# An encoder block on one core: inputs laid out on the host and loaded in fewer pieces, and another order of work at its two ends

## The chip, the cores and the metric

The kernel runs on one core of one Trainium2 chip. A core has a matrix engine (TensorE, PE in the profile, with its weight loads as PEld), a vector engine (VectorE, DVE), an activation engine (ScalarE, ACT), a general engine (GpSimd, POOL) and a sequencer that does little but issue loads and stores (SyncE, SP). ACT and POOL can issue loads too. The metric is the time of one execution on the device in microseconds (us), the median of several runs; less is better.

## The reference

One block of an encoder on a sequence of 256 tokens with 2048 channels, all in float32. Cut to what matters:

```python
hn = rmsnorm(h, mix_norm_pre)                      # h = x at first, (256, 2048)
z, xbc, dt_raw, u = split(hn @ w_in)               # 1024, 1536, 32 and 1024 columns
y_ssd = ssd_mixer(z, xbc, dt_raw, ...)             # centred conv over 5 tokens, scan both ways, gate by z
y_pool = pool_mixer(u, pool_w, pool_scale)         # means over 2, 4, 8, 16 tokens, a linear map
mix = concat([y_ssd, y_pool]) @ w_out
h = h + rmsnorm(mix, mix_norm_post)
ff = conv_glu(rmsnorm(h, ffn_norm_pre), ...)       # 2048 -> 2 x 5632, conv over 3 tokens, gelu, -> 2048
h = h + rmsnorm(ff, ffn_norm_post)
gate = sigmoid(rmsnorm(h, ple_norm_pre) @ w_ple_gate)
return h + rmsnorm(gate * (p @ w_ple), ple_norm_post)
```

`rmsnorm` divides each token's row by the root of its mean square (plus 1e-6) and multiplies each channel by a gain.

## The kernel before

Every product is made of float32 parts. A weight tile is loaded as it is (`raw`), ACT casts it to the format that PE takes (`hi`, line 160), DVE takes the difference (`lo`, line 161), and PE sums three products: x hi by w hi, x hi by w lo, x lo by w hi. `split` (lines 156 to 162) does this; its `hi` and `lo` tiles turn over in five buffers each (`whi`, `wlo`), so that the sixth cast waits for PE to be done with the first. The activations are kept with channels along the partitions in a `Panel`: 16 k-tiles of 128 channels by 256 tokens, `hi` and `lo`, made by `put` (lines 193 to 198: ACT scales by the channel's gain, DVE makes the rest). The row's root is applied behind the product.

The order of work comes from the program's text, with a scheduler that lets later instructions go earlier where their inputs allow; `tc.issue_after` holds one behind another. Nearly all loads are issued on SP's queue, in order, by `load` (lines 115 to 118); one that waits for a buffer holds all behind it. Buffers: `raw` three, `page` (2048 floats a partition) thirteen, `mid` three; PSUM has six banks in `main` and two in `misc`.

The stages, in order:

- Start (lines 92 to 153). POOL makes `ident`, the unit matrix; PE runs nine transposes of it into an unused bank (line 103) while the first loads are under way. `x` is loaded with tokens along the partitions, two token halves, 256 or 512 columns at a time (`xload`), on SP. The gain and convolution vectors are loaded as rows of 128 (`vrow`): one on ACT's queue, nine on POOL's, which also loads `mask`, `dtb`, `alog` and `dsk`. `vturn` transposes the rows on PE and DVE copies them into the columns of `vt`; `vec(i)` is one column.
- `dtu` (lines 346 to 375): the columns of `w_in` for dt and u, 1056 of them, 16 k-tiles. `panel_part` (line 286) transposes `x` on PE, two transposes a k-tile (line 293), and `put` reads the result from PSUM. For each k-tile 18 matmuls of 352 columns go into six banks: two token halves, three products, three column blocks. The raw tiles are `dtur`.
- Row sums and what depends on them (lines 377 to 441): `row_rstd` squares the rows of `x` on ACT; `p` is loaded, transposed on PE and split (`pth`, `ptl`); then dt is made from the first bank by a chain of small DVE instructions that ends in `dah` and `dal` (lines 440, 441).
- `xbc` and `z` (lines 523 to 614): the rest of `w_in`. Between their weight tiles stand the jobs in `work`: `seg_prep` (POOL, products `ap` from `dah`), `seg` (PE and ACT), `pool_mix`, `pool_map` and so on. Each of three slabs of `xbc` ends in a convolution on DVE (line 341).
- The output projection, the feed-forward part (`ga`, `va`, `dna` in the profile) and the small product `ple`.
- The gate (lines 753 to 801): `token_major` with `w_ple_gate`, two halves of 1024 columns. A weight pair is two k-tiles in one load. For all pairs but the last `tail` ones, PE does its matmuls as each pair comes; the last `tail` pairs are done together at the end, bank by bank: first token half 0, then token half 1 (line 226). With `tail = 1 + half` the second half of the columns keeps two pairs, four k-tiles, for this end. Token half 1 has its second bank cut into two of 256 columns, the last one in `gtz`. After each bank: tanh (ACT, line 791), plus one and times `pl` (DVE, 792), square with a sum along the row (ACT, 795), times the gain (DVE, 796). `finish` takes the row's root from POOL (`rms`: one small instruction a partial sum, then a power) and adds `h`: three of four chunks on DVE (line 774), chunk 2 by ACT (771) and POOL (772); each chunk is stored on SP (776).

Of the kernel before, what the change touches and what calls it, by code (L numbers as in the profile page):

```python
# [51 lines left out]
def build(nc, a, out):  # L52
    x, p = a["x"][0], a["p"][0, 0]
# [3 lines left out]

    def rows(ap):
        return ap.rearrange("(n p) -> n p", p=P)

    with tile.TileContext(nc) as tc, \
# [8 lines left out]
        def ins(r):  # L70
            return getattr(r, "ins", r)
# [26 lines left out]
        nc.scalar.activation(tiny("tables", 1), mhalf[:, 0:1], AF.Exp)  # L98
# [3 lines left out]
        for i in range(9):  # L102
            nc.tensor.transpose(warm[:, :P], ident, ident)
        xt = [page(f"x{t}") for t in range(2)]
        vrow = page("vrow")
        vr = vrow[:, :4 * P].rearrange("p (c f) -> p c f", c=4)

        def vload(eng, ch, r0, src, n):
            eng.dma_start(vr[r0:r0 + n, ch, :], src)

        vload(nc.scalar, 0, 0, rows(a["mix_norm_pre"][0]), 16)
# [8 lines left out]
        def xload(c0, c1):  # L120
            for t in range(2):
                last["dma"] = load(xt[t][:, c0:c1], x[t * P:(t + 1) * P, c0:c1])

        xload(0, 256)
        vload(nc.gpsimd, 3, 0, a["ssd_conv_w"][0].rearrange("j (n p) -> (j n) p", p=P), 60)
        vload(nc.gpsimd, 3, 60, rows(a["ssd_conv_b"][0]), 12)
        vload(nc.gpsimd, 3, 72, rows(a["ssd_norm"][0]), 8)
        vload(nc.gpsimd, 3, 80, rows(a["pool_scale"][0]), 8)
        vload(nc.gpsimd, 3, 88, rows(a["ffn_norm_pre"][0]), 16)
        vload(nc.gpsimd, 1, 0, a["ffn_conv_w"][0, 0:2].rearrange("j (n p) -> (j n) p", p=P), 88)  # L130
        vload(nc.gpsimd, 2, 0, rows(a["ffn_conv_w"][0, 2]), 44)
        vload(nc.gpsimd, 2, 44, rows(a["ple_norm_pre"][0]), 16)
        vload(nc.gpsimd, 2, 60, rows(a["ffn_conv_b"][0]), 44)

        mask = ep.tile([P, 4, P], F32, name="mask")
        nc.gpsimd.dma_start(mask, a["masks"].rearrange("m p f -> p m f"))
        vt = cp.tile([P, V_N], F32, name="vt")
        dtb = ep.tile([P, 32], F32, name="dtb")
        alog = ep.tile([P, 32], F32, name="alog")
        dsk = ep.tile([P, H], F32, name="dsk")  # L140
        nc.gpsimd.dma_start(dtb, a["ssd_dt_bias"][0].rearrange("d h -> (d h)").partition_broadcast(P))
        nc.gpsimd.dma_start(alog, a["ssd_a_log"][0].rearrange("d h -> (d h)").partition_broadcast(P))
        nc.gpsimd.dma_start(dsk, a["ssd_d"][0].partition_broadcast(P))

        def vec(i):
            return vt[:, i:i + 1]

        def vturn(ch, c0, n):
            vps = misc(f"vps{ch}")
            nc.tensor.transpose(vps[:, :n], vr[:n, ch, :], ident[:n, :n])  # L150
            nc.vector.tensor_copy(vt[:, c0:c0 + n], vps[:, :n])

        vturn(0, 0, 16)


        def split(name, src, nel):

            hi = wp.tile([P, 1056], F32R, tag="whi", bufs=5, name=f"{name}h")
            lo = wp.tile([P, 1056], F32R, tag="wlo", bufs=5, name=f"{name}l")
            last["act"] = ins(nc.scalar.copy(hi[:, :nel], src))  # L160
            last["dve"] = ins(nc.vector.tensor_sub(lo[:, :nel], src, hi[:, :nel].bitcast(F32)))  # L161
            return hi, lo
# [184 lines left out]
        front = panel_part("hn", hn, xt, V_MIX, 0, 2)  # L347
        for i in range(9):
            nc.tensor.transpose(warm[:, :P], xt[1][:, 128:256], ident)


        c_dt = DSSD + 1536
        for u in range(0, NK, 2):
            if u % 4 == 0 and u:
                panel_part("hn", hn, xt, V_MIX, u, u + 4)
            r = [wp.tile([P, 2048], F32, tag="raw", bufs=3, name=f"dtur{u}"), page(f"dtur{u + 1}")]
            for j in range(2):
                last["dma"] = load(r[j][:, :1056], w_in[(u + j) * P:(u + j + 1) * P, c_dt:c_dt + 1056])
                if u + j == 0:
                    xload(256, 512)  # L360
                    panel_part("hn", hn, xt, V_MIX, 2, 4)
            if u % 4 == 0 and u < 12:
                xload((u + 4) * P, (u + 8) * P)
            for j in range(2):
                k = u + j
                with tc.issue_after(front[0]), tc.issue_after(front[1]):
                    wh, wl = split(f"dtu{k}", r[j][:, :1056], 1056)
                if k == 8:
                    half = last["act"], last["dve"]
                for t in range(2):  # L370
                    xh, xl = (v[:, t * P:(t + 1) * P] for v in hn(k))
                    for q, (xx, ww) in enumerate(((xh, wh), (xh, wl), (xl, wh))):
                        for n in range(3):
                            o = acc2[t][:, :352] if n == 2 else acc[t][n][:, :352]
                            mm(o, xx, ww[:, n * 352:(n + 1) * 352], k == 0 and q == 0, k == NK - 1 and q == 2)

        with tc.issue_after(half[0]), tc.issue_after(half[1]):
            rx = row_rstd("rx", xt)
            vturn(3, 16, 104)
            vturn(1, 120, 88)  # L380
            vturn(2, 208, 104)
# [8 lines left out]
            pt = page("pt")  # L390
            nc.gpsimd.dma_start(pt[:, :512].rearrange("p (t c) -> p t c", t=2), p.rearrange("(t p) c -> p t c", p=P))
            pth = cp.tile([P, 2, L], F32R, name="pth")
            ptl = cp.tile([P, 2, L], F32R, name="ptl")
            ps = misc("ptp")
            for k in range(2):
                for t in range(2):
                    nc.tensor.transpose(ps[:, (2 * k + t) * P:(2 * k + t + 1) * P],
                                        pt[:, t * 256 + k * P:t * 256 + (k + 1) * P], ident)
            pflat = ps.rearrange("p (k t) -> p k t", k=2)
            nc.scalar.copy(pth, pflat)  # L400
            nc.vector.tensor_sub(ptl, pflat, pth.bitcast(F32))
# [360 lines left out]
        ro = {}  # L762

        def finish(t, cs):
            if t not in ro:
                ro[t] = rms(f"go{t}", sq[t], 1.0 / D)
            r = ro[t]
            for c in cs:
                s = slice(c * 512, (c + 1) * 512)
                if c == 2:  # L770
                    nc.scalar.activation(vg[t][:, s], vg[t][:, s], AF.Identity, scale=r)
                    nc.gpsimd.tensor_add(vg[t][:, s], vg[t][:, s], h[t][:, s])
                else:
                    nc.vector.scalar_tensor_tensor(vg[t][:, s], vg[t][:, s], r, h[t][:, s],  # L774
                                                   op0=ALU.mult, op1=ALU.add)
                nc.sync.dma_start(out[t * P:(t + 1) * P, s], vg[t][:, s])
# [44 lines left out]
```

## Time and profile before

| | |
|---|---|
| Median of three runs | 1166.49 us (1166.0 to 1167.83) |
| The profiled execution | 1168.07 us, with a span of 1165.9 us |
| Granted TensorE clock, mean | 0.993 |
| Loads and stores | 216.94 MB, mean 186 GB/s |
| Groups of matmuls of the feed-forward part (`ga`, `va`, `dna`) | share of the chain of waits: 21% each |

The span runs from the first instruction to the last; the execution's time has about 2 us around it. A group in the profile is named by its line, engine, operation and tiles ("out<-in" by the program's names), with how often it ran. Line 89 is the matmul helper, so matmuls are told apart by their tiles. A time in a timeline is counted from the start of the span; a row has its start, its length, the engine, the line, the operation and, in brackets, how long the engine was idle before and what ended that. A length with "xN" covers N instructions in a row. Matmuls are pipelined: each has a latency longer than the step to the next, so steps are taken from starts.

### The profile page before, as it was taken

To read this page: it belongs to the slowest core of one execution; us is meant where nothing else is said; L and a number is where in the kernel's file an instruction comes from. 1 tells how busy PE (TensorE), PEld (TensorE's weight loads), DVE (VectorE), ACT (ScalarE), POOL (GpSimd) and SP (SyncE) were. 2 spreads that over 40 slices of the span, in tenths; PEclk is the share of its full clock that TensorE was granted. 3 is DMA by queue.
4 is the path that set the end of the run, shared out by engine and by line. 5 is a ranking of instruction groups with operands and counts; after the bars stand their busy time and mean duration, and the time that the engine had idled before them with its cause. 6 is when DMAs were issued, how large, how long until landed. Compare 5 with 4: busy or idle time off the path is not lost.

```text
span 1165.9 us, 15412 instructions
## 1 busy us (share of the span) xinstructions
PE 1143.7 (98%) x6138; PEld 984.0 (84%) x6138; DVE 755.4 (65%) x933; ACT 576.6 (49%) x774; POOL 132.9 (11%) x138
## 2 busy tenths in 40 slices
PE   8998999999999999999999999999999999999995
PEld 8997988888888888888888888888888888887885
DVE  4579797655777665665766756656555565557554
ACT  4634543454575554544544544544444454447453
POOL 2165404300110000000000000000000000001002
PEclk9998999999999999999999999999999999999998
DMA  9653337555465565555555555566566556654742
GB/s 312 239 206 109 109 111 261 208 180 190 134 217 181 188 195 194 182 180 185 194 194 186 181 183 192 183 205 213 182 193 198 185 183 194 198 183 145 248 149 73
DMA packets 129591, 216.94 MB, mean 186 GB/s; under 512 B 3896, under 2 KB 96722, under 8 KB 128880
## 3 DMA queue, kind: packets, MB, share of 16 engines
q1 hardware_dynamic: 128944, 215.23, 56.4%
q0 software_dynamic: 544, 0.72, 0.4%
q8 instruction: 48, 0.79, 0.3%
q14 instruction: 23, 0.19, 0.0%
q10 hardware_dynamic: 32, 0.01, 0.0%
HBM read 213.85 MB, written 2.10 MB: 185 GB/s over the span
## 4 chain that ended last, share of the span: by engine, by line
PE 91%; DVE 5%; ACT 1%; DMA 1%; POOL 1%; issue 1%; SPq 0%; DVEq 0%; POOLq 0%; ACTq 0%
PE va L89 21%; PE dna L89 21%; PE ga L89 21%; PE woa L89 8%; PE gt L89 7%; PE z L89 4%; PE xbc L89 3%; PE dtu L89 3%; DVE cv L341 2%; DMA dtur<-w_in 1%; DVE w L542 1%; DVE xb_0l L161 0%; PE ple L89 0%; PE yd L89 0%; DVE vg L774 0%
## 5 line engine op out<-in xcount | busy, mean ns | idle before, releaser
L89 PE MATMUL ga<-wox,ug_0h 128*128 128x512 f32 x352 | 126.2, 396 | 0.0
L89 PE MATMUL ga<-wox,ug_1h 128*128 128x512 f32 x352 | 125.8, 395 | 0.0
L89 PE MATMUL va<-wox,uv_0h 128*128 128x512 f32 x352 | 125.5, 395 | 0.0
L89 PE MATMUL va<-wox,uv_1h 128*128 128x512 f32 x352 | 125.5, 395 | 0.0
L89 PE MATMUL dna<-dn_1h,hs 128*128 128x512 f32 x352 | 104.5, 394 | 0.0
L89 PE MATMUL dna<-dn_0h,hs 128*128 128x512 f32 x352 | 104.5, 393 | 0.0
L89 PE MATMUL ga<-wox,ug_1l 128*128 128x256 f32 x352 | 99.0, 281 | 0.0
L89 PE MATMUL ga<-wox,ug_0l 128*128 128x256 f32 x352 | 99.0, 281 | 0.0
L89 PE MATMUL va<-wox,uv_0l 128*128 128x256 f32 x352 | 98.9, 281 | 0.0
L89 PE MATMUL va<-wox,uv_1l 128*128 128x256 f32 x352 | 98.9, 281 | 0.0
L89 PEld LDWEIGHTS va<-wox,uv_1h 128*128 128x128 f32 x352 | 66.1, 188 | 15.7
L89 PEld LDWEIGHTS va<-wox,uv_0h 128*128 128x128 f32 x352 | 66.1, 188 | 15.7
L89 PEld LDWEIGHTS ga<-wox,ug_1h 128*128 128x128 f32 x352 | 66.1, 188 | 15.5
L89 PEld LDWEIGHTS ga<-wox,ug_0h 128*128 128x128 f32 x352 | 66.1, 188 | 15.5
L89 PEld LDWEIGHTS dna<-dn_1h,hs 128*128 128x128 f32 x352 | 66.2, 188 | 15.2
L89 PEld LDWEIGHTS dna<-dn_0h,hs 128*128 128x128 f32 x352 | 66.1, 188 | 15.2
L719 POOL TENSOR_TENSOR fc<-fc,rfb 128x1024 f32<-128x1024 f32 x11 | 26.4, 2404 | 443.0 <-ACT fc L718 443.0
L89 PEld LDWEIGHTS ga<-wox,ug_0l 128*128 128x128 f32 x352 | 66.4, 189 | 0.1
L89 PEld LDWEIGHTS ga<-wox,ug_1l 128*128 128x128 f32 x352 | 66.4, 189 | 0.0
L89 PEld LDWEIGHTS va<-wox,uv_1l 128*128 128x128 f32 x352 | 66.4, 189 | 0.0
L89 PEld LDWEIGHTS va<-wox,uv_0l 128*128 128x128 f32 x352 | 66.4, 189 | 0.0
L735 ACT CAST hs<-hid 128x512 fp32r<-128x512 f32 x44 | 27.3, 620 | 71.0 <-PE dna L89 70.7
(644 smaller groups left out, 2674.1 us busy)
## 6 DMA issues: line engine op xcount, KB each, us to landing
dn0r<-w_ffn_down SPq DMA_DIRECT2D x22, 1024.0 KB, 5.4
dn1r<-w_ffn_down SPq DMA_DIRECT2D x22, 1024.0 KB, 5.5
dtur<-w_in SPq DMA_DIRECT2D x16, 528.0 KB, 8.7
zr<-w_in SPq DMA_DIRECT2D x8, 1024.0 KB, 5.1
wo0r<-w_out SPq DMA_DIRECT2D x8, 1024.0 KB, 5.7
wo1r<-w_out SPq DMA_DIRECT2D x8, 1024.0 KB, 5.5
gt0r<-w_ple_gate SPq DMA_DIRECT2D x8, 1024.0 KB, 5.5
gt1r<-w_ple_gate SPq DMA_DIRECT2D x8, 1024.0 KB, 5.5
```

The costliest lines, as they stand in the source:

```text
L89: nc.tensor.matmul(o, lhsT, rhs, start=start, stop=stop, skip_group_check=True)
L341: nc.vector.scalar_tensor_tensor(o[:, lo:hi], i[:, lo + d:hi + d], vec(wcol + j * wstep + f), o[:, lo:hi], op0=ALU.mult, op1=ALU.add)
L542: nc.vector.scalar_tensor_tensor(w[:, h * P:(h + 1) * P], cbm[:, 0, g, t, :], dt[:, t, 8 * g + h:8 * g + h + 1], w[:, h * P:(h + 1) * P], ...
L719: nc.gpsimd.tensor_tensor(cv.rearrange("p (f t) -> p f t", f=4), cv.rearrange("p (f t) -> p f t", f=4), rfb.unsqueeze(1).to_broadcast([P, ...
L735: nc.scalar.copy(t[:, :512], src)
```

## The change

At the start, a host function `laid_out` puts three arrays together by copying: `x_cols`, the 16 gains of the first norm and then `x` transposed into k-tiles of 128 channels by 256 tokens; `p_t`, `p` transposed; `columns`, the other vectors as columns, then `dtb`, `alog`, `dsk` repeated over the partitions, then the four masks. The kernel loads them on SP in few loads (`xt`, `vt`, `small`, `pt`); the `vrow` rows, their transposes, the transposes of `x` (`panel_part` here) and of `p`, and POOL's loads are gone. The row sums load `x` a second time, with tokens along the partitions (`xs_`), behind the last `dtu` weight tile. Weight tile 0 comes in three pieces, two of them issued first on ACT's queue ahead of ACT's table load, the third on SP; tile 1 comes in two. Their casts and differences are cut likewise (`cuts`). For k-tile 0 the matmuls go product by product over both token halves. The warm-up transposes are 16 in place of 9, and the nine behind the first `x` are gone.

At the end, the second half of the gate keeps four pairs in place of two (`1 + 3 * half`); four of those eight k-tiles take their `hi` and `lo` from four pages (`spare`). All final adds are on DVE. For token half 1 POOL sums the partial sums ahead of the last one, takes the root (`rest_of`) and writes it beside the last piece's values, so that the last square's sum is the whole mean square; then one power remains.

```diff
+        c_dt = DSSD + 1536
+        r0 = wp.tile([P, 2048], F32, tag="raw", bufs=3, name="dtur0")
+        for n in range(2):
+            first = ins(nc.scalar.dma_start(r0[:, n * 352:(n + 1) * 352],
+                                            w_in[:P, c_dt + n * 352:c_dt + (n + 1) * 352]))
+        with tc.issue_after(first):
+            nc.scalar.activation(tiny("tables", 1), mhalf[:, 0:1], AF.Exp)
...
-        for i in range(9):
+        for i in range(16):
             nc.tensor.transpose(warm[:, :P], ident, ident)
...
-        vload(nc.gpsimd, 3, 0, a["ssd_conv_w"][0].rearrange("j (n p) -> (j n) p", p=P), 60)
...
-        nc.gpsimd.dma_start(mask, a["masks"].rearrange("m p f -> p m f"))
...
+        last["dma"] = load(xt[0], a["x_cols"][:, :V_SCW + L])
+        dtb, alog, dsk = small[:, :32], small[:, 32:64], small[:, 64:80]
+        mask = small[:, 80:].rearrange("p (m f) -> p m f", m=4)
...
+            for c0, c1 in zip((0, *cuts), (*cuts, nel)):
+                s = slice(c0, c1)
+                last["act"] = ins(nc.scalar.copy(hi[:, s], src[:, s]))
+                last["dve"] = ins(nc.vector.tensor_sub(lo[:, s], src[:, s], hi[:, s].bitcast(F32)))
...
-        front = panel_part("hn", hn, xt, V_MIX, 0, 2)
-        for i in range(9):
-            nc.tensor.transpose(warm[:, :P], xt[1][:, 128:256], ident)
+        def x_panel(k0, k1):
+            for k in range(k0, k1):
+                done = put(hn(k), x_part(k), vec(V_MIX + k))
+            return done
+        front = x_panel(0, 1)
...
+                if k == 0:
+                    last["dma"] = load(r[0][:, 704:1056], w_in[:P, c_dt + 704:c_dt + 1056])
+                    xload(1, 2)
+                    x_panel(1, 2)
+                    continue
+                for c0, c1 in ((0, 704), (704, 1056)) if k == 1 else ((0, 1056),):
+                    last["dma"] = load(r[j][:, c0:c1], w_in[k * P:(k + 1) * P, c_dt + c0:c_dt + c1])
+                if k == 1:
+                    xload(2, 4)
+                elif k in (3, 5, 7):
+                    xload(*{3: (4, 9), 5: (9, 13), 7: (13, 16)}[k])
+                elif k == 4:
+                    load(vt, a["columns"][:, :V_N - V_SCW])
+                elif k == 6:
+                    load(small, a["columns"][:, V_N - V_SCW:])
...
-            rx = row_rstd("rx", xt)
+            xs_ = [page(f"x{t}") for t in range(2)]
+            for t in range(2):
+                load(xs_[t], x[t * P:(t + 1) * P, :])
+            rx = row_rstd("rx", xs_)
...
+        def rest_of(o):
+            base = EPS * D
+            for n, q in enumerate(sq[1]):
+                m = tiny(f"go1m{n}", 1)
+                nc.gpsimd.tensor_scalar(m, q, 1.0, base, op0=ALU.mult, op1=ALU.add)
+                base = m
+            nc.gpsimd.tensor_tensor(o, m, half_up, op=ALU.pow)
...
-                if c == 2:
-                    nc.scalar.activation(vg[t][:, s], vg[t][:, s], AF.Identity, scale=r)
-                    nc.gpsimd.tensor_add(vg[t][:, s], vg[t][:, s], h[t][:, s])
-                else:
-                    nc.vector.scalar_tensor_tensor(vg[t][:, s], vg[t][:, s], r, h[t][:, s],
-                                                   op0=ALU.mult, op1=ALU.add)
+                nc.vector.scalar_tensor_tensor(vg[t][:, s], vg[t][:, s], r, h[t][:, s],
+                                               op0=ALU.mult, op1=ALU.add)
...
+                for i in (8, 6):
+                    sh, sl = page(f"gth{i}", F32R), page(f"gtl{i}", F32R)
+                    for j in range(2):
+                        spare[f"gt1{NK - i}_{j}"] = (sh[:, j * 1024:(j + 1) * 1024], sl[:, j * 1024:(j + 1) * 1024])
-            token_major(f"gt{half}", w_gate, half * 1024, list(range(NK)), hp, acc, 1 + half)
+            token_major(f"gt{half}", w_gate, half * 1024, list(range(NK)), hp, acc, 1 + 3 * half)
```

More of the change, by code (lines that the diff above doesn't have):

```diff
@@ L56, in build @@
     out = out[0]
-    def rows(ap):
-        return ap.rearrange("(n p) -> n p", p=P)
     with tile.TileContext(nc) as tc, \
@@ L138, in build @@
[L138 to L143, printed above, removed]
-        def vec(i):
[L146 to L161, printed above, removed]
+        def x_part(k):
+            return xt[0][:, V_SCW:] if k == 0 else xt[1 + k // 9][:, (k - 1) % 8 * L:((k - 1) % 8 + 1) * L]
@@ L790, in build @@
                     v = th[:, :c1 - c0]
+                    end = half == t == 1 and c1 == 1024
+                    if end:
+                        rest_of(th[:, c1 - c0:c1 - c0 + 1])
                     nc.scalar.activation(v, o, AF.Tanh, scale=rh[t])
```

134 lines of the change are left out of this document (70 added, 64 removed).

## The prediction

> **What bounds the kernel now.** I read the page first, for where the time lies; then the chain of work that ended last, in order of time, because the change touches only the first 60 us and the last 35; then the timelines and the busy time by window of those two ends.
>
> ```profile
> span 1165.9 us, 15412 instructions
> ...
> PE 1143.7 (98%) x6138; PEld 984.0 (84%) x6138; DVE 755.4 (65%) x933; ACT 576.6 (49%) x774; POOL 132.9 (11%) x138
> ```
>
> TensorE (PE) is busy for 98% of the span. So there are two ways to gain: matmuls taken away, and time at either end in which PE waits or has already finished.
>
> ```profile
> 5.46 12.10 DMA dtur<-w_in
> ...
> 43.33 16.45 PE dtu L89 x102
> ...
> 91.29 12.65 DVE cv L341 x15
> ```
>
> In this chain (start, length, what) the first stage, `dtu`, is late once, for the load of its fourth weight tile; then PE runs it alone up to 43.33 + 16.45 = 59.78. Here 102 matmuls take 16.45 us, 0.161 us each; the stage has 16 x 18 = 288 of them, 46.4 us. Much later a convolution on VectorE (DVE) comes on the path.
>
> ```profile
> 0.73 0.86 SPq L118 DMA_DIRECT2D x<-x  x2
> ...
> 1.31 0.79 POOL L109 DMA_DIRECT2D vrow<-ssd_conv_w  x1 [0.34 <-issue]
> ...
> 2.21 0.32 POOL masks.py:199 TENSOR_SCALAR_AFFINE_SELECT ident<-ident 128x128 f32<-128x128 f32 x1
> ...
> 2.58 2.18 PE L103 MATMUL dtu<-ident 128*128 128x128 f32 x9 [2.58 <-POOL ident masks.py:199]
> ...
> 6.61 1.07 ACT L160 CAST dtu0h<-dtur 128x1056 fp32r<-128x1056 f32 x1
> ...
> 7.74 1.24 PE L89 MATMUL dtu<-dtu0h,hnh 128*128 128x352 f32 x6
> ```
>
> This is the timeline of the start. The first useful matmul is at 7.74, behind the load and the whole cast of tile 0. From 7.74 to 59.78 are 52.0 us for 46.4 us of matmuls; the other 5.6 are transposes and waits.
>
> ```profile
> L293 PE MATMUL hnt<-ident,x 128*128 128x128 f32 x32 | 5.9, 295 | 0.0
> ...
> L196 ACT ACTIVATE hnh<-hnt,vt 128x256 fp32r<-128x256 f32 x16 | 7.4, 473 | 17.0 <-PE hnt L293 15.4 <-DVE hnl L197 1.4
> ```
>
> **The change part by part: the front.** All 32 transposes of `x` go, and with them four of `vrow` and four of `p`. Eight of the 32 stand ahead of 7.74, so 24 leave the stage; that is 24 x 0.11 = 2.6 us of the 5.6, by this row of the timeline, (1.03 - 0.295)/7 a step:
>
> ```profile
> 34.25 1.03 PE L293 MATMUL hnt<-ident,x 128*128 128x128 f32 x8
> ```
>
> The other 3.0 are waits for tiles 3 and 4 and for the ScalarE (ACT) step behind the transposes.
>
> When can the first matmul run? It needs `x` tile 0 (136 KB with the gains) and, piece by piece, weight tile 0.
>
> ```profile
> dtur<-w_in SPq DMA_DIRECT2D x1, 528.0 KB, 4.9
> x<-x SPq DMA_DIRECT2D x2, 128.0 KB, 2.5
> ```
>
> Two 128 KB loads landed 2.5 us after issue, the tile issued third, at about 1.6, after 4.9: 784 KB were in by 6.5. Now 664 KB are wanted, and two pieces are issued on ACT's queue beside SP's, so `x` lands at about 3.5 to 4, the third piece between 4.6 (at the 353 GB/s of the window 4 to 6 us, shown below) and 5.9. An ACT step of 0.47 and three casts of a third of 1.07 follow; each is done about 0.4 after its piece. PE is ready before that: POOL no longer issues a load of 0.79 us ahead of the mask that makes `ident`, so the 16 warm-ups, at (2.18 - 0.43)/8 = 0.22 each, end near 5.1 (at 6.1, if `ident` were as late as now). I take 5.8 for the start that the stage would have had if it never waited, between 5.0 and 6.8.
>
> Does it then run through? Up to weight tile 15 the queue carries 16 x 528 KB, 2 MB of `x` and 0.45 MB of vectors and masks: 11.2 million bytes.
>
> ```profile
> 4.00:6.00 2.00, 2.00 (x10) 1.63 (x9) 0.17 (x1) 0.00 (x0) 2.00 (x4) 1.00 1.02 353
> ...
> 14.00:16.00 2.00, 2.00 (x15) 1.98 (x15) 1.64 (x2) 0.71 (x2) 0.00 (x0) 1.00 0.98 113
> ...
> 2.00:18.00 16.00, 15.29 (x88) 13.86 (x88) 6.58 (x10) 6.61 (x12) 6.87 (x14) 1.00 0.99 293
> 18.00:26.00 8.00, 6.75 (x40) 6.44 (x41) 4.48 (x5) 4.61 (x6) 0.00 (x0) 1.00 1.03 410
> ```
>
> The last column is GB/s, the one before it the DMA engines' busy share. At 14 to 16 us they are busy and move almost nothing: the short rows of `mask`, `dtb`, `alog`, `dsk` from POOL's queue are in flight. Once these are through, 410 hold, `x` loads among them. The change merges the short rows into rows of 1 to 5 KB. Even at the 293 of the bad stretch, tile 2 (2.15 MB in the queue's order) is there at 9.4, tile 4 (3.9 MB) at 15.3, tile 7 at 24.2, tile 15 at 40.3. PE wants tile k at 5.8 + 2.9k: 11.6, 17.4, 26.1, 49.3. A cast of 1.07 fits in each time; the tightest is tile 7, by 0.8. ACT has 0.47 + 1.07 = 1.54 us of work for each tile against PE's 2.9, and DVE has the same two steps. The second copy of `x`, 2 MB for the row sums, is queued behind tile 15; ACT's square over it stands ahead of the cast of tile 15, and at 293 GB/s its first half is there at 44. So the stage ends at 5.8 + 46.4 = 52.2 in place of 59.8: **7.6 us**, bounds 6.5 and 8.4.
>
> **The stage behind it.** What matters is not PE alone.
>
> ```profile
> 68.98 0.20 DVE L440 CAST dah<-da 128x64 fp32r<-128x64 f32 x1
> ...
> 91.22 13.45 DVE L341 SCALAR_TENSOR_TENSOR cv<-xr,vt,cv 128x254 f32<-128x254 f32 x16
> ...
> 133.41 6.39 DVE L341 SCALAR_TENSOR_TENSOR cv<-xr,vt,cv 128x254 f32<-128x254 f32 x16
> ```
>
> ```profile
> 69.26 1.07 POOL L465 TENSOR_TENSOR ap<-dah,mask 128x512 fp32r<-128x512 f32 x1 [13.67 <-DVE dah L440]
> 70.31 2.01 POOL L465 TENSOR_TENSOR ap<-dal,mask 128x512 fp32r<-128x512 f32 x1
> ...
> 101.20 1.22 POOL L465 TENSOR_TENSOR ap<-dal,mask 128x512 fp32r<-128x512 f32 x1
> ```
>
> The first convolution runs beside POOL's `ap` products and takes 13.45 us, the second mostly without them 6.39; PE then waits for a PSUM bank that DVE frees behind it:
>
> ```profile
> PE seg L89 <- DVE catl L197: 4.1, 1, 4.1
> ```
>
> After the change the chain to `dah` has two more weight subtractions (`xb`) in front of it, the last of which waits for PE: `dah` comes some 11.8 us after the end of `dtu`, not 9.4, and POOL starts 2.4 later. But the two subtractions that met POOL's first products, two long ones (2.01 against 1.07), are over by then: 2 us back. POOL ends about 0.4 later against the end of `dtu`, the convolution starts 0.8 earlier (seven transposes of 0.11 gone behind `dtu`), and ends where it did. I take 0 here: DVE's chain, and all behind it, moves forward with the end of `dtu`. PE's wait grows by the 0.8 us that it saved. Bounds: 3.9 lost, 4.0 gained (rivals).
>
> **The tail.** PE has the same matmuls in another order, so its end stays; only what follows counts. In the tail the first token half stands ahead of the second; with eight tiles in it in place of four, PE finishes that half 24 matmuls of 512 columns earlier:
>
> ```profile
> 1142.84 5.55 PE gt L89 x24
> ```
>
> Its work on ACT, DVE and POOL moves 5.5 us ahead with it, out of the way of the second half.
>
> ```profile
> 1151.71 1.42 DVE L774 SCALAR_TENSOR_TENSOR vg<-vg,go0r,h 128x512 f32<-128x512 f32 x2 [1.15 <-POOL go0r L283]
> ...
> 1153.69 0.28 PE L89 MATMUL gtz<-gt_1h,dnxl 128*128 128x256 f32 x1
> ...
> 1155.47 0.45 ACT L791 ACTIVATE gth<-gtz,rh 128x256 f32<-128x256 f32 x1
> ...
> 1156.79 0.42 DVE L792 SCALAR_TENSOR_TENSOR gth<-gth,pl 128x256 f32<-128x256 f32 x1
> ...
> 1157.24 0.42 ACT L795 ACTIVATE gth<-gth 128x256 f32<-128x256 f32 x1 [0.28 <-DVE gth L792]
> ...
> 1157.56 0.19 ACT L795 ACTIVATION_READ_ACCUMULATOR gth<-gth 128x1 f32 x1
> ...
> 1158.26 0.55 POOL L283 TENSOR_TENSOR go1r<-go1m,mhalf 128x1 f32<-128x1 f32 x1
> 1158.85 3.08 DVE L774 SCALAR_TENSOR_TENSOR vg<-vg,go1r,h 128x512 f32<-128x512 f32 x3 [1.19 <-POOL go1r L283]
> ```
>
> PE ends at 1153.97, but the last tanh starts at 1155.47, behind DVE's and ACT's work on half 0. Freed of it: tanh 1154.01 to 1154.46, multiply to 1154.90, square and its read (0.33 + 0.19) to 1155.46, POOL's power at 1155.62 (the last sum is folded into the square), to 1156.17, then four adds on DVE at 1.42/2 = 0.71: end 1159.05. Now it is 1158.85 + 3.08 = 1161.93. **2.9 us**, bounds 2.3 and 3.1. POOL's sum of the earlier squares and its root hide behind PE's last 2.8 us (24 matmuls of half the columns); without that cover they would cost the power's 0.55 and more. The casts of the four pairs held back cost nothing: four of the eight tiles go to pages that do not wait for PE, a cast costs about 1.07 and a tile's matmuls 12 x 0.231 = 2.8, and the last of the eight is wanted 7 x 3 x 0.231 = 4.9 us into the tail.
>
> **Sum.** 7.6 + 0 + 2.9 = 10.5. The profiled execution, 1168.07 with a span of 1165.9, would become 1157.6 with a span of 1155.4; it is 1.6 above the median of 1166.49, so for the median **1156.0**, 1153.6 to 1158.2 by the bounds of front and tail with 1 us for the draw.
>
> **The rivals.**
> (a) POOL's later start is not won back: the convolution ends 2.4 us later, PE's wait passes 6 us, and PE is slow afterwards for longer:
>
> ```profile
> 102.40:109.60 7.20, 3.10 (x27) 2.90 (x25) 7.05 (x13) 2.89 (x6) 0.01 (x1) 0.94 0.36 114
> 109.60:116.00 6.40, 6.37 (x20) 5.32 (x21) 4.00 (x9) 2.79 (x5) 1.87 (x1) 0.54 0.60 199
> ```
>
> Behind the wait the granted clock (third column from the right) is 0.54 for 6.4 us, a loss of 2.9; half as much again makes 2.4 + 1.5 = 3.9 lost: **1159.9**. For it: the order of DVE's work. Against: the contention removed.
> (b) The wait shrinks by a us instead and the slow clock does not come: 1.1 + 2.9 = 4.0 gained, **1152.0**. Against it: PE arrives earlier, not later. [...]
> (c) Slower: the short rows were not what held the DMA engines, and the mixture of `x` and weights moves no faster than about 180 GB/s through the whole first stage. Place: ACT's casts waiting for `dtur`. Tile 15 then lands at 2 + 62 = 64, the stage ends at about 69: 17 lost against 52.2, **1173**. It decides below 200 GB/s, where tile 15 would come at 58 and all 10.5 us would be gone. For it: the 113. Against: the 410.
> (d) The reordered tail does nothing, since adds and stores end as late as now: 7.6 alone, **1158.9**. Against: the row at 1155.47.
>
> **How the numbers follow.** Forecast 0.72, (a) 0.11, (b) 0.07, (c) 0.05, (d) 0.05. The range 1152.6 to 1160.2 takes in (d) and most of (a); it leaves out (c), most of (b), the far side of (a) and the edges of the forecast, under 2 in 10. A measurement of this kernel can tell 0.2%, 2.3 us, from no change: forecast, (a), (b) and (d) lie beyond it, 0.94 with a little taken off; within it 0.02; slower 0.04.
>
> **What would show it.** No `hnt`; the first `dtu` matmul near 5.5 and its last near 52; no idle time of ACT on `dtur` above 0.5 us after tile 1; GB/s above 350 at 6 to 18; PE's wait at `seg` 4 to 6 us; the last add about 5 us behind PE's last matmul, not 8. It would be wrong if `dtu` ended after 54, or if the wait at `seg` passed 7.

## The result, and the profile after

| | median | lowest to highest | runs |
|---|---|---|---|
| before | 1166.24 us | 1165.36 to 1167.83 | 4 |
| after | 1154.71 us | 1153.95 to 1155.9 | 4 |

The ratio is 0.9901, 95% interval 0.9883 to 0.9918: 11.5 us less by the medians, where 10.5 were forecast. The page of the changed kernel:

```profile
span 1152.5 us, 15287 instructions
...
PE 1134.8 (98%) x6096; PEld 978.4 (85%) x6096; DVE 753.5 (65%) x934; ACT 574.7 (50%) x775; POOL 121.4 (11%) x123
```

PE's busy time fell by 8.9 us with 42 instructions fewer; at 0.11 us for a transpose that would be 4.6, so something else became faster too. The chain of waits in order of time (start, length, what):

```profile
1.16 3.77 DMA dtur<-w_in
4.95 0.49 ACT dtu0h L147
5.49 46.88 PE dtu L86 x287
52.37 0.44 PE rxbp L86 x4
...
83.67 13.44 DVE cv L328 x15
```

`dtu` runs without a stop from 5.49 to 52.37 (before: to 59.78). The 15 instructions of the convolution that stand in this chain take 13.44 us; before they took 12.65. The end of the timeline:

```profile
1143.01 0.55 POOL L771 TENSOR_TENSOR gth<-go1m,half_up 128x1 f32<-128x1 f32 x1
...
1143.49 0.28 PE L86 MATMUL gtz<-gt_1h,dnxl 128*128 128x256 f32 x1
1143.87 0.47 ACT L806 ACTIVATE gth<-gtz,rh 128x256 f32<-128x256 f32 x1 [1.38 <-PE gtz L86]
1144.38 0.42 DVE L807 SCALAR_TENSOR_TENSOR gth<-gth,pl 128x256 f32<-128x256 f32 x1 [1.97 <-ACT gth L806]
1144.90 0.42 ACT L812 ACTIVATE gth<-gth 128x257 f32<-128x257 f32 x1 [0.55 <-DVE gth L807]
1145.48 0.55 POOL L776 TENSOR_TENSOR go1r<-gq,mhalf 128x1 f32<-128x1 f32 x1 [1.92 <-ACT gth L812]
1146.07 2.74 DVE L781 SCALAR_TENSOR_TENSOR vg<-vg,go1r,h 128x512 f32<-128x512 f32 x4 [0.81 <-POOL go1r L776]
```

The last tanh follows PE's last matmul at once (1143.49 + 0.28, then 1143.87), POOL's root of the earlier sums is done before it, and the adds end at 1148.81, 5.04 us behind PE; before it was 7.96.

To place the whole difference, the starts of the first matmul of each stage (PE's timeline) stand side by side. The kernel before was profiled a second time, later (E10 below), because the first execution was 1.6 us above its median:

| starts at (us) | before, 1168.07 | before again, 1165.87 | after, 1154.53 | after minus before again, by stage |
|---|---|---|---|---|
| `xbc` (so `dtu` is done) | 59.74 | 58.66 | 52.57 | -6.1 |
| `z` | 159.37 | 157.25 | 152.01 | +0.85 in `xbc` |
| output projection | 215.58 | 213.40 | 208.30 | +0.1 |
| feed-forward, `ga` | 312.46 | 310.25 | 305.33 | +0.2 |
| `dna` | 810.84 | 808.64 | 800.74 | **-3.0** in `ga` and `va` |
| last gate matmul | 1153.69 | 1151.50 | 1143.49 | -0.1 |
| end of the span | 1165.9 | 1163.7 | 1152.5 | -3.2 |

The sum is -11.2. The forecast had -7.6, 0 and -2.9: the front gave less, and 3 us came from a stage that the prediction never looked at.

### The profile page after: what moved, and what is told of

It is laid out like the page before. It is cut to its first block, busy times and chain, and to the rows that moved or that the text cites. A ratio compares the mean times of both kernels' runs of the same rounds, so it can differ in the third digit from the quotient of the medians.

```text
span 1152.5 us, 15287 instructions
## 1 busy us (share of the span) xinstructions
PE 1134.8 (98%) x6096; PEld 978.4 (85%) x6096; DVE 753.5 (65%) x934; ACT 574.7 (50%) x775; POOL 121.4 (11%) x123
## 4 chain that ended last, share of the span: by engine, by line
PE 92%; DVE 5%; ACT 1%; issue 1%; POOL 1%; DMA 0%; DVEq 0%; POOLq 0%; ACTq 0%
PE va L86 21%; PE dna L86 21%; PE ga L86 21%; PE woa L86 8%; PE gt L86 7%; PE dtu L86 4%; PE z L86 4%; PE xbc L86 3%; DVE cv L328 2%; DVE w L541 1%; DVE xb_0l L148 1%; PE ple L86 0%; PE yd L86 0%; DVE h L677 0%; DMA dtur<-w_in 0%
## 5 line engine op out<-in xcount | busy, mean ns | idle before, releaser
L86 PEld LDWEIGHTS ga<-wox,ug_0l 128*128 128x128 f32 x352 | 66.2, 188 | 0.1
L86 PEld LDWEIGHTS ga<-wox,ug_1l 128*128 128x128 f32 x352 | 66.2, 188 | 0.0
L86 PEld LDWEIGHTS va<-wox,uv_1l 128*128 128x128 f32 x352 | 66.2, 188 | 0.0
L86 PEld LDWEIGHTS va<-wox,uv_0l 128*128 128x128 f32 x352 | 66.2, 188 | 0.0
```

The lines of the kernel that those rows point to most:

```text
L86: nc.tensor.matmul(o, lhsT, rhs, start=start, stop=stop, skip_group_check=True)
```

## The experiments

Each time is a median; the ratio is to the kernel before, run beside it on the same chip, with its 95% interval. Diffs are against the changed kernel unless said.

**E1, the changed start with the old end.**

```diff
+                if c == 2:
+                    nc.scalar.activation(vg[t][:, s], vg[t][:, s], AF.Identity, scale=r)
+                    nc.gpsimd.tensor_add(vg[t][:, s], vg[t][:, s], h[t][:, s])
...
-            token_major(f"gt{half}", w_gate, half * 1024, list(range(NK)), hp, acc, 1 + 3 * half)
+            token_major(f"gt{half}", w_gate, half * 1024, list(range(NK)), hp, acc, 1 + half)
```

> The changed start with the end of the kernel before. By the prediction's sum it keeps the front's 7.6 us and none of the tail's 2.9: about 1158.6 against 1166.2 for the kernel before; the last add ends about 8 us behind PE's last matmul. By a rival, the 2.8 us by which the two traces differ in the feed-forward stage (128 matmuls in 22.33 us there instead of 22.47, which the prediction did not have) belong to the front, for example by where the buffers lie: then about 1156 and 22.33 in this trace too. If it is a draw of the one profiled execution, the pace in this trace lies anywhere between 22.3 and 22.5 and the time is 1158.6.

1157.47 us, ratio 0.9922 (0.9908 to 0.9935), 9.1 us less than the 1166.61 of before beside it. PE ends at 1144.83, the last add at 1152.76, 7.9 later. So the start alone brings more than the 7.6 of the forecast, but not where it was forecast: the feed-forward part runs 3.0 us faster here too (495.4 us from its first matmul to `dna`, 498.4 before), which leaves 6.1 for the front.

**E2, the old start with the new end** (before, with `rest_of`, `spare` and `1 + 3 * half`).

> The kernel before with the changed end. By the prediction's sum 2.9 us less than before, about 1163.3, with the last add about 5 us behind PE's last matmul. By rival (d) of the prediction nothing: 1166.2. If the pace of the feed-forward stage hangs on the four pages that the tail takes, about 1160.5 and 22.33 us for 128 matmuls of that stage.

1163.1 us, ratio 0.9971 (0.996 to 0.9983), 3.5 less. PE ends at 1151.35, the adds at 1156.38, 5.0 behind; the feed-forward part keeps the pace of before. The tail's 2.9 stand, and the 3 us of the feed-forward part belong to the start.

**E4, the short rows back.** The thirteen loads of vectors, masks and the dt constants go back to POOL's queue, in short rows; the vector rows are loaded beside `vt` and not read.

```diff
+            vload(nc.gpsimd, 3, 0, a["ssd_conv_w"][0].rearrange("j (n p) -> (j n) p", p=P), 60)
...
+            nc.gpsimd.dma_start(mask, a["masks"].rearrange("m p f -> p m f"))
...
-                elif k == 6:
-                    load(small, a["columns"][:, V_N - V_SCW:])
```

> The changed kernel with the 13 loads of short rows back on POOL's queue (mask, dtb, alog and dsk are read from there, the vector rows are loaded and not read; the load of small is gone). Theory of the prediction: the short rows held the DMA engines in the first 18 us; a window of 2 us below 250 GB/s comes back between 8 and 18 us, a weight tile is late, and dtu ends at 53.5 to 57 instead of 52.4: 1 to 4 us more than the changed kernel. Rival: they were harmless and the slump came from the loads of x with tokens along the partitions: above 390 GB/s throughout from 8 us on, the same time within 0.5 us.

1157.27 us, ratio 0.993 (0.9916 to 0.9943): 2.6 slower than the change. Busy time by window (columns: stretch, its length, busy time of PE, PEld, DVE, ACT, POOL with instructions, granted clock, busy share of the DMA engines, GB/s), first of E4, then of the changed kernel:

```profile
12.00:14.00 2.00, 1.59 (x10) 1.37 (x9) 1.52 (x2) 1.02 (x1) 0.00 (x0) 1.00 1.24 269
14.00:16.00 2.00, 2.00 (x15) 2.00 (x14) 0.38 (x2) 0.62 (x2) 0.00 (x0) 1.00 0.84 147
```

```profile
6.00:8.00 2.00, 2.00 (x13) 2.00 (x14) 1.24 (x3) 1.40 (x3) 0.00 (x0) 1.00 1.02 307
8.00:10.00 2.00, 2.00 (x14) 2.00 (x13) 1.70 (x4) 1.27 (x3) 0.00 (x0) 1.00 1.02 411
...
14.00:16.00 2.00, 2.00 (x14) 2.00 (x13) 1.67 (x4) 1.55 (x3) 0.00 (x0) 1.00 1.02 417
```

With these loads the slump is back, 147 GB/s against 417 at 14 to 16 us, PE stops in `dtu`, and the stage ends at 55.08. In that window 31 packets of POOL's queue, 0.01 MB, take 44.3% of the engines' time, and 117 packets of SP's queue, 0.29 MB, take 39.8% (in the kernel before it is 36 packets of POOL's queue and 69.2%). So what the prediction read from one window of before, that these loads hold the DMA engines, is shown, at 2.6 us by the medians. Whether it is the length of their rows, POOL's queue, or that `dtb`, `alog` and `dsk` send one row to all partitions, was not tried apart.

**E5, weight tiles 0 and 1 whole, on SP's queue.**

```diff
-                    last["dma"] = load(r[0][:, 704:1056], w_in[:P, c_dt + 704:c_dt + 1056])
+                    last["dma"] = load(r[0][:, :1056], w_in[:P, c_dt:c_dt + 1056])
...
-                    wh, wl = split(f"dtu{k}", r[j][:, :1056], 1056, ((352, 704), (704,))[k] if k < 2 else ())
+                    wh, wl = split(f"dtu{k}", r[j][:, :1056], 1056)
```

> The changed kernel with weight tiles 0 and 1 each in one load on SP and each cast whole. By the prediction tile 0 is then there at about 4.6 to 5.5, its cast of 1.07 us ends near 6.3, and the stage dtu ends 0.4 to 1.2 us later than in the changed kernel (52.4): 52.8 to 53.6, and as much more time. Rival: the pieces are worth nothing, since the next tiles set the pace: 52.4. Rival: the later start makes tile 1 or 2 late too: above 54.

1155.94 us, ratio 0.9909 (0.9894 to 0.9924): 1.2 slower than the change. The timelines of E5 and then of the changed kernel show why:

```profile
5.09 1.07 ACT L142 CAST dtu0h<-dtur 128x1056 fp32r<-128x1056 f32 x1 [1.59 <-DMA dtur<-w_in]
...
6.21 2.13 PE L86 MATMUL dtu<-dtu0h,hnh 128*128 128x352 f32 x6 [1.16 <-ACT dtu0h L142]
```

```profile
4.19 0.47 ACT L147 CAST dtu0h<-dtur 128x352 fp32r<-128x352 f32 x1
...
4.72 2.07 PE L86 MATMUL dtu<-dtu0h,hnh 128*128 128x352 f32 x6
4.95 0.87 ACT L147 CAST dtu0h<-dtur 128x352 fp32r<-128x352 f32 x2 [0.29 <-DMA dtur<-w_in]
```

The pieces let PE begin 1.5 us earlier, and it then waits once for the next piece. In this execution `xbc` begins at 54.84, 2.3 later than in the changed kernel and more than I had expected. The part beyond 1.5 looks like a draw of the execution: the first matmuls of E5 come at 0.29 to 0.32 us a step up to 9.9 us, those of the changed kernel at 0.16 from 6.6 on, and E6 below has the same slow beginning with the start of the change untouched. So the size stays uncertain: 1.2 by the medians, with intervals that overlap.

**E3, `pool_map` and `cb` one place later** in the `xbc` work list, meant to shorten the wait behind the convolution.

```diff
-            [job(seg_prep, 4), job(seg, 1), job(pool_map, 0), job(pool_map, 1)],
-            [job(seg_prep, 5), job(seg, 2), job(cb, bc, 0), job(cb, bc, 1)],
+            [job(seg_prep, 4), job(seg, 1)],
+            [job(seg_prep, 5), job(seg, 2), job(pool_map, 0), job(pool_map, 1)],
```

> The changed kernel with pool_map and cb each moved one place later in the list of jobs. Theory: PE's 5.0 us wait at seg is for a PSUM bank that pool_map filled and that DVE frees only behind the first convolution (14.2 us long); with pool_map behind seg the wait falls below 1.5 us and at least one of the two windows of half clock behind it goes: 4 to 8 us less than the changed kernel, 1147 to 1151. Rival: DVE is the bound there whatever PE does next, the wait reappears at the xbc matmuls, whose weight difference stands behind the same convolution: 1153 to 1155. Second rival: the wait goes but the half clock stays: about 1151.

1158.11 us, ratio 0.9927 (0.9914 to 0.9939): 3.4 slower than the change. PE's waits in this stage (who <- for whom: us in total, times, longest), E3 and then the changed kernel:

```profile
PE pw L86 <- ACT E L473: 7.5, 1, 7.5
PE pw L86 <- DVE catl L184: 2.2, 1, 2.2
```

```profile
PE seg L86 <- DVE catl L184: 5.0, 1, 5.0
```

The wait only moved, and grew: `pw` now stands behind `seg`'s exponential on ACT, which is queued behind a step that needs the convolution. The convolution itself took longer, 17.37 us in place of the changed kernel's 14.23, with POOL's products beside it up to 100.96 in place of 95.96, and ended 3.4 later. My theory fell: the wait follows DVE's convolution wherever PE's jobs stand.

**E6, two pairs held back in place of four,** with the new adds and the folded sum kept (`1 + half`, no `spare`).

> The changed kernel with two pairs held back in the gate's second half, as before, and all else of the new end kept (adds on DVE, last sum folded into the square). Theory: the four pairs are worth the 1.0 to 1.5 us by which the last tanh stood behind PE before; here the last add ends 6 to 6.6 us behind PE's last matmul instead of 5.0, 1.0 to 1.5 us more time. Rival: with chunk 2 off ACT and POOL the last tanh is free anyway: 5.0 and no difference. Second rival: DVE, with all adds, is later still: over 7.

1158.28 us, ratio 0.9929 (0.9914 to 0.9944): 3.6 slower than the change, about as slow as the whole old end (E1). Its timeline, by engine:

```profile
1143.04 2.75 DVE L781 SCALAR_TENSOR_TENSOR vg<-vg,go0r,h 128x512 f32<-128x512 f32 x4 [1.15 <-POOL go0r L270]
```

```profile
1147.31 1.27 POOL L769 TENSOR_SCALAR go1m<-gq,go1m 128x1 f32<-128x1 f32 x2 [3.39 <-ACT gth L810]
...
1149.26 0.42 ACT L808 ACTIVATE gth<-gth 128x257 f32<-128x257 f32 x1 [1.72 <-POOL gth L771]
...
1150.43 2.74 DVE L781 SCALAR_TENSOR_TENSOR vg<-vg,go1r,h 128x512 f32<-128x512 f32 x4 [1.98 <-POOL go1r L776]
```

PE ends at 1145.33 and the adds 7.8 later. The adds of token half 0 run up to PE's end, ahead of half 1's work on DVE; in the changed kernel they are over 5 us before that:

```profile
1135.93 2.75 DVE L781 SCALAR_TENSOR_TENSOR vg<-vg,go0r,h 128x512 f32<-128x512 f32 x4 [1.15 <-POOL go0r L270]
```

Half 1's squares come late in E6, POOL's two sums and the root no longer lie under PE's last matmuls, and the last square waits 1.72 us for them. That is the cover that the prediction named; without it the fold and the adds on DVE gain nothing. The tail accounts for 2.8 of the 3.6 us. In this profile `dtu` also ends later, at 54.15 in place of 52.37, with the same start:

```profile
L86 PE MATMUL dtu<-dtu0l,hnh x6: 482/495/495, 7.8 to 9.3; 128*128 128x352 f32 x6
L86 PE MATMUL dtu<-dtu0h,hnl x6: 320/323/352, 9.6 to 10.4; 128*128 128x352 f32 x6
```

Up to 9.6 us its matmuls come at half the later pace, (9.3 - 7.8)/5 = 0.30 us a step, then (10.4 - 9.6)/5 = 0.16; in the changed kernel's profile the same six of `dtu0l` start from 6.6 to 7.4, 0.16 us a step.

**E8, the changed kernel with the weight buffers in the order of before.** The build chooses which of the five `hi` and five `lo` buffers each weight tile takes. Counted by address in the built program (the traces name tiles, not places) they come in the order 0 4 3 1 2 and 0 4 1 2 3 before, and 0 4 3 2 1 for both after. E8 writes the old order out:

```diff
+                n = turn.setdefault("n", 0) % 5
+                turn["n"] += 1
+                hi = turn["hi"][:, (0, 4, 3, 1, 2)[n] * 1056:((0, 4, 3, 1, 2)[n] + 1) * 1056]
+                lo = turn["lo"][:, (0, 4, 1, 2, 3)[n] * 1056:((0, 4, 1, 2, 3)[n] + 1) * 1056]
```

> The changed kernel with the five buffers of weight parts turned over by hand in the order that the kernel before has them in the feed-forward stage (hi 0 4 3 1 2, lo 0 4 1 2 3) instead of the changed kernel's (0 4 3 2 1 both); all other buffers lie where they were. Theory formed after the first four runs: the step from matmul to matmul there goes by the weight buffer, not by the panel's page, and the order alone makes the stage 2.9 us longer: 498.2 us from the first matmul of ga to the last of va instead of 495.3, about 1157.6 in all. Rival: pages or addresses of something else make it: 495.3 and 1154.7.

1158.15 us, ratio 0.9931 (0.9914 to 0.9947): 3.4 slower. The matmuls of `va` by tile (duration in ns: least, median, most; first and last start), of before, after and E8:

```profile
L89 PE MATMUL va<-wox,uv_0h x352: 387/395/404, 338.9 to 807.7; 128*128 128x512 f32 x176
...
L89 PE MATMUL va<-wox,uv_1h x352: 387/395/404, 341.7 to 810.5; 128*128 128x512 f32 x176
```

```profile
L86 PE MATMUL va<-wox,uv_0h x352: 387/392/401, 331.7 to 797.6; 128*128 128x512 f32 x176
...
L86 PE MATMUL va<-wox,uv_1h x352: 387/392/401, 334.5 to 800.4; 128*128 128x512 f32 x176
```

```profile
L86 PE MATMUL va<-wox,whi x704: 387/395/403, 332.7 to 804.3; 128*128 128x512 f32 x176
```

First to last start: 471.6 us before, 468.7 after, 471.6 again in E8. The last two differ in the places of the weights, and in that E8 cuts its buffers by hand out of one tile; E11 below does that too and keeps the fast pace, so the places make the difference. This is the 3.0 us that the forecast lacks.

**E7, the convolution without POOL beside it:** POOL's `ap` products from the fifth group on wait for the first convolution, that of slab 2.

```diff
+            if slab == 2:
+                last["held"] = ins(nc.gpsimd.tensor_copy(tiny("held", 1), cv[:, 1023:1024]))
...
+                with tc.issue_after(last["held"]) if i >= 4 else nullcontext():
```

> The changed kernel with POOL's products ap from the fifth group on held back until the first convolution has ended (a copy of one of its columns stands ahead of them on POOL). Theory: the convolution is slow (14.2 us for 16 instructions, 0.89 each) because POOL works beside it; alone an instruction takes 0.4 to 0.5 and it ends 4 to 6 us earlier, PE's wait of 5.0 us at seg falls below 1.5 and the half clock behind it comes for at most one window: 4 to 8 us less than the changed kernel, 1147 to 1151. Rival: the convolution takes as long without POOL: no difference, 1154 to 1156. Second rival: the ap products, now late, become the next wait: seg waits for POOL, 1154 to 1160.

1154.57 us, ratio 0.9898 (0.9883 to 0.9913): no different from the change. E7's timeline and its waits:

```profile
83.42 7.96 DVE L328 SCALAR_TENSOR_TENSOR cv<-xr,vt,cv 128x254 f32<-128x254 f32 x16
...
107.13 7.70 DVE L544 SCALAR_TENSOR_TENSOR w<-cbm,dt,w 128x128 f32<-128x128 f32 x8 [4.53 <-POOL w L539]
```

```profile
PE seg L86 <- DVE catl L184: 4.2, 1, 4.2
```

The changed kernel's timeline has the same convolution as

```profile
83.59 14.23 DVE L328 SCALAR_TENSOR_TENSOR cv<-xr,vt,cv 128x254 f32<-128x254 f32 x16
```

It falls from 14.2 to 8.0 us and the old wait is gone, but POOL's held products now meet the next work of DVE: eight `w` products (`cbm` times `dt`) take 7.70 us, and PE waits 4.2 at a later `seg`.

**E9 and E11, on top of E7.** E9 moves all four `pool_map` jobs into the `z` stage; E11 is E9 with the weight buffers in rising order for `hi` and `lo` alike.

```diff
+            [job(pool_map, 0), job(pool_map, 1)],
+            [job(pool_map, 2), job(pool_map, 3)],
```

> The kernel of e7 (the first convolution without POOL beside it) with all four pool_map jobs moved to the stage z, so that no PSUM bank that PE wants waits for DVE. Theory: in e7 the gain was given back 19 us later, where PE waits 4.5 us for a pool_map bank behind DVE's w products, slow beside POOL's next ap products. Without pool_map there, PE waits at most 1.5 us in a row between 75 and 150 us and no window of half clock follows: 5 to 9 us less than the changed kernel, 1146 to 1150. Rival: the wait moves once more, to the xbc matmuls, whose weight difference stands behind w on DVE: 1152 to 1155.

> The kernel of e9 with the five weight buffers turned over in rising order (0 1 2 3 4, hi and lo alike) instead of 0 4 3 2 1. Theory: it is the order alone that sets the step in the feed-forward stage; which order is fast isn't known. If every step there took the 229.3 ns of the three fast buffers, the stage would take about 493.5 us in place of 495.3; at the slow end 499. Rival: only that hi and lo have the same order matters: 495.3.

E9: 1162.85 us (0.9969, 0.9958 to 0.9981), 8.1 slower than the change: without these jobs PE waits 4.5 us in `xbc` for a weight difference and 3.5 behind the next convolution, so `xbc` falls only from 99.4 to 97.8 us, while `z`, where PE had waited 0.2 us, takes in their matmuls and grows from 56.3 to 66.2. E11: 1163.11 us (0.9971, 0.9961 to 0.9981), the same as E9. Its `va` row:

```profile
L86 PE MATMUL va<-wox,whi x704: 387/392/401, 340.0 to 808.7; 128*128 128x512 f32 x176
```

468.7 us again. So 0 4 3 2 1 is not the only order that gives this pace; in both that do, `hi` and `lo` go round alike.

**E10, the kernel before once more,** unchanged, for a second profile.

> The kernel before once more, for another execution with a profile. Theory: the 1168.07 of the profile shown first lay 1.6 to 1.8 above its median because of late weight tiles in dtu; here dtu ends at 57.8 to 59 instead of 59.8, the feed-forward stage takes 498.2 us again and the time is 1165.5 to 1167. Rival: the stage always ends at 59.8 and the front of the change is worth the 7.4 us of the first pair of traces.

1166.45 us (ratio 1.0, 0.999 to 1.001); its profiled execution took 1165.87. Busy time by window (columns as above), E10 and then the changed kernel:

```profile
105.00:108.00 3.00, 0.00 (x0) 0.00 (x0) 2.85 (x5) 1.04 (x4) 0.00 (x0) 1.00 0.69 205
108.00:111.00 3.00, 2.44 (x8) 2.03 (x9) 2.56 (x4) 2.66 (x4) 0.00 (x0) 0.77 0.37 144
111.00:114.00 3.00, 3.00 (x14) 2.55 (x14) 1.87 (x7) 0.55 (x2) 1.85 (x1) 0.66 0.78 233
114.00:117.00 3.00, 3.00 (x27) 3.00 (x27) 2.96 (x12) 1.61 (x4) 0.05 (x1) 1.00 0.33 122
```

```profile
99.00:102.00 3.00, 0.00 (x0) 0.00 (x0) 3.00 (x4) 1.04 (x3) 0.00 (x0) 0.80 0.59 164
102.00:105.00 3.00, 2.20 (x5) 1.82 (x6) 2.40 (x5) 2.52 (x5) 0.00 (x0) 0.50 0.48 186
105.00:108.00 3.00, 3.00 (x10) 2.37 (x9) 1.34 (x3) 0.76 (x2) 0.70 (x1) 0.56 0.67 180
108.00:111.00 3.00, 3.00 (x28) 3.00 (x27) 2.94 (x13) 1.04 (x4) 1.19 (x1) 1.00 0.44 169
```

In stretches of 0.5 us the granted clock of the changed kernel from 95 to 113 us is 1.00 or 0.50, except in the two where it changes (0.81 and 0.86); in the first profile of before, from 100 to 118 us, it is so too (0.66 and 0.51). With these two values, time at half clock is the shortfall times two: (0.23 + 0.34) x 3 x 2 = 3.4 us in E10, which is what the expectations call one window of half clock, and (0.20 + 0.50 + 0.44) x 3 x 2 = 6.8 in the changed kernel, their two windows. The first profile of before had the long form too: (0.06 x 7.2 + 0.46 x 6.4) x 2 = 6.8. Against this second profile the front gives 6.1 and `xbc` loses 0.85; against the first, which had the long form as the changed kernel has, `xbc` gains 0.2 (99.63 and 99.44 us).

**E12, the `w` products kept clear as well:** E7, and POOL's last two groups of `ap` wait until `w` is made.

```diff
+        def hold():
+            last["held"] = ins(nc.gpsimd.tensor_copy(tiny("held2", 1), ee[0][:, 1023:1024]))
...
-            [job(seg_prep, 6), job(seg, 3), job(pool_map, 2), job(pool_map, 3)],
-            [job(seg_prep, 7), job(seg, 4), job(weigh, 0, 0)],
+            [job(seg, 3), job(pool_map, 2), job(pool_map, 3)],
+            [job(seg, 4), job(weigh, 0, 0), job(hold), job(seg_prep, 6), job(seg_prep, 7)],
```

> The kernel of e7 with POOL's seventh and eighth group of products ap also held back, until DVE has made the first quarter of E with w (a copy of one of its columns stands ahead of them, and w itself goes ahead of both on POOL); pool_map stays where it was. Theory: in e7 DVE's eight w products took 7.7 us beside POOL's ap instead of 2.2, and the wait of 4.5 us behind them ate what the first convolution had won. Alone they take about 2.2; PE's longest wait between 75 and 150 us falls below 2 us, with no window of half clock or one: 4 to 8 us less than the changed kernel, 1147 to 1151. Rival: the held products come too late in turn, PE waits at seg for POOL or at the second convolution: 1153 to 1158.

**1151.32 us** (1151.1 to 1151.58), ratio 0.9868 (0.9852 to 0.9885): 3.4 us below the change, the fastest of all. E12's timeline:

```profile
84.03 7.96 DVE L328 SCALAR_TENSOR_TENSOR cv<-xr,vt,cv 128x254 f32<-128x254 f32 x16
...
107.13 2.19 DVE L544 SCALAR_TENSOR_TENSOR w<-cbm,dt,w 128x128 f32<-128x128 f32 x8 [3.08 <-POOL w L539]
...
120.50 8.74 DVE L328 SCALAR_TENSOR_TENSOR cv<-xr,vt,cv 128x254 f32<-128x254 f32 x16
```

The eight `w` products are back at 2.19 us, no wait at `seg` is left, and `xbc` takes 95.8 us in place of 99.4. It gained a little less than I had expected: the groups held back now meet the next convolution (8.74 us; 6.39 in the kernel before), and PE waits 2.5 us there.

## Why the prediction was right, and where its steps were not

The time came out 1.3 us under the forecast and inside its range, but two errors of opposite sign stand behind that: the front's term was 1.5 too large, and 3.0 us of the feed-forward part were missing. That the sum came so near is in part luck.

- **Front, 7.6 forecast.** The new end of `dtu` was right: 52.2 forecast, 52.37 measured. So were the start near 5.5 (PE began at 4.72 and ran through from 5.49) and the loads on POOL's queue as the cause of the slump. What failed is what the gain was counted against: I took 59.78, the end of `dtu` in one execution, and then took 1.6 off the total because that execution was above the median. With the old start `xbc` begins at 59.74 there, but at 58.66 in E10 and 58.28 in E2; so 1.1 or more of late tiles, which the change removes, were counted twice. Against the second profile the term is 6.1. The new start varies too: in eight profiles `xbc` begins at 52.4 to 53.0, in E6 at 54.35. E4 puts 2.6 of the 6.1 on the merged loads and E5 about 1.2 on the pieces; the remaining 2.3 lie near the 2.6 reckoned for 24 transposes, which were not tried by themselves.
- **Middle, 0 forecast.** `dah` was ready 12.15 us behind `dtu` (11.8 forecast, 9.4 before), and PE's wait grew from 4.1 to 5.0 (4.9 forecast). The steps that should have won POOL's later start back came only in part. POOL's last product ended 1.0 later against the end of `dtu`, not 0.4. The convolution started 0.2 earlier, not 0.8, took 14.23 us in place of 13.45, and ended 0.6 later instead of where it did. The 0.85 lost against the second profile can't be put down to that, because the length of the half clock differs between executions: in the kernel before, behind the same wait of 4.1 us, it was 6.8 us in the first profile and 3.4 in E10. With 6.8 us of it `xbc` took 99.63 us before and 99.44, 99.35, 98.99 and 99.02 in the changed kernel, E1, E5 and E6; with 3.4 us it took 98.59 (E10) and 98.54 (E2) before and 98.48 in E4 (E8, with the old order of the weights, took 100.13 with 6.8). Like against like the 0 holds. Whether the longer wait makes the long form likelier is open: it came in five of six profiles with the new wait and in one of three with the old.
- **Feed-forward, not in the sum.** The prediction took PE's matmuls there as fixed, and so left out -3.0 us. The missing step was to look at what else the edit moves: with the new start (E1 has the faster pace, E2 has not) the build turns the weight buffers over in another order. `dtu` has 16 weight tiles in both kernels, and what in the start changes the order was not found. With the order of before (E8) the change takes 1158.15, at the upper edge of the forecast's own 1153.6 to 1158.2; the new order, which nobody had aimed at, took 3 us off that.
- **Tail, 2.9 forecast.** 2.9 measured at the last add (7.96 to 5.04), 0.3 more at the stores. Each step of the chain came as listed, and E6 shows that the cover by PE's last matmuls is a condition.
- **Rivals.** (a) did not come: the wait stayed at 5.0 and the convolution's end moved by 0.6 us. (b) did not come: the wait grew, from 4.1 us to 5.0, and the half clock did not go away. That a wait of about 3 us would be free of it was my estimate, which no run shows; in E12 3.4 us of it followed a wait of 2.5. (c) did not come: the loads on POOL's queue were what held the engines, and taking them away is worth 2.6 (E4). (d) did not come (E2: 3.5).
- **Signs that failed without harm.** ACT did stand idle for tiles 6 and 7 (1.48 and 2.13 us) and the first window carried 307 GB/s, not 350. PE did not stop, since casts were still ahead of it.

## What to carry to other kernels

An execution's surplus over the median lies somewhere; find the stage before you subtract it, and do not also count its removal as the change's gain. Compare the pace of the stages that an edit does not touch as well: here a quarter of the gain came from there, because the weights lay elsewhere. Where one engine's work is slower beside another's (here DVE's convolution, 14.23 us beside POOL's products and 7.96 with the later ones held back), keep them apart in time over the whole stretch: PE's longest wait fell from 5.0 us to 2.5 in E12, while moving one job only moved the wait (E3: 7.5; E7: 4.2).

## What the runs showed of the hardware

- **The pace of the matmuls of `ga` and `va` went with the place of their weights.** From the starts of the 1408 matmuls of 512 columns of `ga` and `va`, the mean step to the next start, by the five turns of the weight buffers: before 233.3, 232.9, 232.9, 229.8, 236.6 ns; after 229.5, 229.1, 232.6, 229.4, 232.4; E8 233.1, 232.7, 232.8, 229.7, 236.4; E11 229.3, 232.6, 229.5, 232.6, 229.3. In the changed kernel and in E11 buffers 1 and 3 have the longer step, at whatever turn they stand; in the old order four of the five turns have a longer one. That the old order, in which `hi` and `lo` go round differently, costs 3 us is shown; what makes a buffer's step longer is open.
- **DVE beside POOL.** A convolution instruction took 14.23/16 = 0.89 us beside POOL's products in the changed kernel and 7.96/16 = 0.50 in E7; a `w` product 7.70/8 = 0.96 beside them in E7 and 2.19/8 = 0.27 clear of them in E12. These rows show what it cost, not the cause; that the cost moved with POOL's work, from the convolution to the `w` products, is shown by E7.
- **Half clock after a short wait.** In E12 PE stood idle only from about 131.2 to 133.7, yet (0.15 + 0.42) x 3 x 2 = 3.4 us at half clock followed:

```profile
133.00:136.00 3.00, 2.28 (x17) 2.29 (x18) 3.00 (x4) 1.19 (x2) 1.94 (x1) 0.85 0.58 235
136.00:139.00 3.00, 3.00 (x17) 3.00 (x17) 3.00 (x9) 0.00 (x0) 0.32 (x1) 0.58 0.00 0
```

In E3 PE stood idle for 2.2 us at 128.5, and no slow stretch followed. After 4.1 us of wait it was 6.8 us once (before) and 3.4 twice (E10, E2); after 4.9 to 5.0 it was 6.8 five times (the changed kernel, E1, E5, E6, E8) and 3.4 once (E4). So the same wait was followed by 3.4 us at half clock or by 6.8. A wait of 2.5 us was enough once (E12) and one of 2.2 us was not (E3); what decides between none, 3.4 and 6.8 us is open.
